# Reordering RWKV's last third and its transposes, one decay multiply, and an identity added on VectorE

## The chip, the cores and the metric

The kernel runs on one core of a Trainium2 chip. The metric is the device time of one execution in microseconds (us), as the median of several. TensorE (PE in the profile) does the matrix products, VectorE (DVE), ScalarE (ACT) and GpSimd (POOL) the rest of the arithmetic; SyncE (SP) only issues transfers.

## What is computed

One layer of a hybrid block over 2048 latent tokens and 256 context tokens, width 1024. An input projection feeds two groups of heads: a bidirectional RWKV-7 mixer with 8 heads of 64, and a multi-head attention with 8 heads. Their gated outputs go through one output projection and are added to the residual stream. The part that the change touches is the RWKV scan, in the reference a loop over tokens, once forward and once backward:

```
def step(S, inp):
    r_t, w_t, k_t, v_t, a_t, b_t = inp
    sa = jnp.einsum('bhij,bhj->bhi', S, a_t)
    S = S * w_t[:, :, None, :] + sa[..., None] * b_t[:, :, None, :] + v_t[..., None] * k_t[:, :, None, :]
    y = jnp.einsum('bhij,bhj->bhi', S, r_t) if emit else None
    return S, y
```

The state of each head is a 64 x 64 matrix; every token decays it (w), applies a delta rule (a, b), adds an outer product (v, k) and reads it out (r).

## The kernel before

The kernel has an input stage (projection, preparation of keys and decays, all stored to DRAM), a stage that projects queries, keys and values for the attention, the attention itself, and the output projection with a final norm.

The RWKV scan is done in 36 chunks of 64 tokens, both directions in one pass (the forward direction in one half of the partitions, the backward one in the other). Within a chunk the token loop is replaced by products: scores between the chunk's keys and receivers (`scores`), the inverse of a unit triangular matrix of 64 x 64 for each head and direction (`inverse`, built by levels with small f16 products), and a chain that carries the state from chunk to chunk (`chain1`, `chain1b`, `chain2`, `chain3`, `chain4`). `transposed` turns a chunk's decayed keys by TensorE transposes against the identity.

This work is laid beside the attention. The attention runs 16 jobs (4 pairs of heads by 4 groups of 512 queries) of 9 macro steps each. A macro step does, for j = 0 to 3, three score products into PSUM (L1426 to L1428), the exponential on ScalarE (L1430), an addition on GpSimd (L1435), some products and maxima for the next job (L1306 on TensorE, L1307 on VectorE), and then one slot of RWKV work (`slot`); after j = 3 a fifth slot follows at once. At its end it calls `tiled`, which is handed the eight products of the step's probabilities with the values (`pv`, L1453) as the function `between`. Three macro steps make one chunk: `tiled` does `chain1`, the second half of the scores and `chain1b` at the end of the first (m = 0), `chain2` at the end of the second (m = 1), `chain3`, `chain4` and the first half of the scores of a later chunk at the end of the last (m = 2). The first 18 macro steps run beside the projection for the attention, and the remaining 99 beside the attention proper.

The inverse of a chunk is a generator; one of its steps runs at each of the slot numbers listed in `STAGES`. Two chunks' inverses overlap. In the first three of its product steps it forms T (here called T0, T1 and T2): T0 in slot 2 of a second macro step, T1 in slot 4 of the same step (right ahead of `between` and `chain2`), T2 in slot 1 of the last macro step. Each is a product of the lower-order matrix with the T before it, plus the identity. The identity comes in through one more product, `self.idt` times `self.id8` (128 x 512, L327), that opens the accumulation in PSUM, and ScalarE copies the sum out (L358). The last inverse step of the older chunk, which makes `Rf` (L393 on VectorE), is in slot 3 of the second macro step, between T0 and T1; `chain2` multiplies by `Rf` (L432).

In the last macro step slot 3 holds the first `level` step (products at L330, two VectorE multiplications at L347), slot 4 another product and its VectorE addition (L370), and `chain3` (products at L446) follows. `chain3` adds to the state on VectorE (L449) and multiplies it by the chunk's decay, one operation for each direction (L451); `chain4` (products at L462) makes the chunk's output (L463).

TensorE's order is the order of the program text (`phase_core` runs under a manual schedule of TensorE). The order of the other engines' queues is made when the program is built, and each queue is then worked through in that order. Products of the inverse and of the chain take their PSUM space from the two banks named "x" (`BANKS`); scores of the attention and the maxima share the three banks named "s". `transposed`, the first half of the scores and `chain1` share one tile of two banks ("bc").

Of the kernel before, what the change touches and what calls it, by code (L numbers as in the profile page):

```python
# [12 lines left out]
ALU = mybir.AluOpType  # L13
# [4 lines left out]
P = 128  # L18
# [52 lines left out]
def bc(ap, n):  # L71

    return ap.unsqueeze(len(ap.shape)).to_broadcast(list(ap.shape) + [n])
# [66 lines left out]
class Rwkv:  # L140
# [67 lines left out]
    def tiled(self, k, between=None):  # L208

        n, m = divmod(k, 3)  # L210
        n -= 3
        ok = lambda i: 0 <= i < self.NC
        between = between or (lambda: None)
        if m == 0:
            between()
            if ok(n):
                self.chain1(n)
            if ok(n + 2):
                self.scores(n + 2, 1)
                self.inv[n + 2] = self.inverse(n + 2)  # L220
                next(self.inv[n + 2])
            if ok(n):
                self.chain1b(n)
            if ok(n + 3):
                self.load_ar(n + 3)
                self.load_bk(n + 3)
        elif m == 1:
            between()
            if ok(n):
                self.chain2(n)  # L230
        else:
            if ok(n):
                self.chain3(n)
                self.chain4(n)
            between()
            if ok(n + 3):
                self.scores(n + 3, 0)

# [42 lines left out]
    def transposed(self, n):  # L281
        nc = self.nc
        tr = self.S[n]["tr"] = []
        pb = self.k.banks.tile([P, 2, 512], F32, name="bc")
        for d in range(2):
            ps = pb[:, d]
            for b in range(4):
                nc.tensor.transpose(ps[:, b * P:(b + 1) * P], self.bk[:, d, b].rearrange("p j t -> p (j t)"), self.k.ident)
            t = self.op.tile([P, 512], F32, name=f"tr{d}", bufs=3)
            (nc.vector.tensor_copy if d else nc.scalar.copy)(t, ps)  # L290
            tr.append(t)

    def scores(self, n, d):
# [24 lines left out]
    def inverse(self, n):  # L318

        nc, s, op, par = self.nc, self.S[n], self.op, n % 2  # L320

        ph, pl = self.bd[f"ph{n % 3}"], self.bd[f"g{par}"]

        def prod(lhsT, rhs, also=None, plus=None):
            ps = self.k.bank("x").rearrange("p (h t) -> p h t", t=64)
            if plus is not None:
                nc.tensor.matmul(ps, self.idt, plus, start=True, stop=False)  # L327
            for h in range(8):
                r = rhs[:, h] if len(rhs.shape) == 3 else rhs
                nc.tensor.matmul(ps[:, h], lhsT[:, h], r, start=plus is None,  # L330
                                 stop=also is None and (plus is None or h == 7))
                if also is not None:
                    nc.tensor.matmul(ps[:, h], also[:, h], r, start=False, stop=plus is None or h == 7)
            return ps

        def packed(name, bufs):
            return op.tile([P, 8, 64], F16, name=f"{name}{par}", bufs=bufs)

        def spread(name, x, both=None):
            for d, ur, vr in self.dirs:  # L340
                (nc.vector.tensor_copy if d and not both else nc.scalar.copy)(self.bd[name][ur, :, ur], x[ur])
            return self.bd[name]

        def level(name, x, i):

            for d, ur, vr in self.dirs:
                nc.vector.tensor_tensor(self.bd[name][ur, :, ur], x[ur],  # L347
                                        self.lvl[ur, i, ur].unsqueeze(1).to_broadcast([64, 8, 64]), op=ALU.mult)
            return self.bd[name]

        pm = op.tile([P, 8, P], F16, name=f"pm{par}")
        nc.vector.tensor_tensor(pm, ph, self.lv8(0), op=ALU.mult)
        T = None
        yield 1
        for i in range(3):
            ps = prod(pm, T if i else self.id64, plus=self.id8)
            T = packed("T", 2)
            nc.scalar.copy(T, ps)  # L358
            if i == 2:
                Dm = packed("D", 1)  # L360
                nc.vector.transpose(Dm, T)
            yield 1
        for lev in (1, 2):
            G = level(f"g{par}", prod(ph, T), lev)
            yield 1
            R = Dm
            for i in range(3):
                ps = prod(G, R)
                R = packed("R", 4)
                nc.vector.tensor_tensor(R, ps, Dm, op=ALU.add)  # L370
                if i == 2:
                    Dm = R
                    if lev == 1:
                        T = packed("T", 2)
                        nc.vector.transpose(T, R)
                    else:
                        Rb = spread("f", R, both=True)
                        for d, ur, vr in self.dirs:
                            nc.gpsimd.tensor_tensor(pl[ur, :, ur], s["sm"][d][ur, :, ur], ph[ur, :, ur],
                                                    op=ALU.subtract)  # L380
                yield 1
        ps = prod(Rb, self.id64)
        T = packed("T", 2)
        nc.scalar.copy(T, ps)
        im = op.tile([P, 8, 64], F16, name="im")
        nc.gpsimd.tensor_tensor(im, self.id8, T, op=ALU.subtract)
        yield 1

        Fb = spread("f", prod(ph, T, also=pl, plus=im))
        yield 1  # L390
        ps = prod(Fb, R)
        Rf = s["R"] = op.tile([P, 8, 64], F32, name="Rf", bufs=2)
        nc.vector.tensor_tensor(Rf, ps, R, op=ALU.add)  # L393
        yield 1
# [41 lines left out]
    def chain3(self, n):  # L436

        nc, s = self.nc, self.S[n]
        if n + 1 >= self.NC:
            return  # L440
        ps = self.k.bank("x").rearrange("p (d b t) -> p d b t", d=2, t=64)
        for b in range(4):
            for d in range(2):
                for hb in range(2):
                    c = slice(64 * (2 * b + hb), 64 * (2 * b + hb) + 64)
                    nc.tensor.matmul(ps[64 * hb:64 * hb + 64, d, b], s["tr"][d][:, c], s["uv"][d][:, c],  # L446
                                     start=True, stop=True)
        st, st2 = self.ST[n % 2], self.ST[(n + 1) % 2]
        nc.vector.tensor_tensor(st2, ps, st, op=ALU.add)  # L449
        for d in range(2):  # L450
            nc.vector.tensor_tensor(st2[:, d], st2[:, d], bc(s["gg"][:, d], 64), op=ALU.mult)  # L451

    def chain4(self, n):

# [1238 lines left out]
```

## Time and profile before

| what | value |
|---|---|
| median of 3 runs | 3074.02 us (3060.97 to 3078.2) |
| the profiled execution's own time | 3086.14 us |
| its span, first to last instruction | 3084.4 us |
| TensorE busy | 2732.8 us, 89% |
| VectorE busy | 1836.6 us, 60% |
| GpSimd busy | 1384.8 us, 45% |
| ScalarE busy | 1287.7 us, 42% |
| mean granted TensorE clock | 0.942 |

The busy time of an engine is the union of its instructions' times. A matrix product's end is modelled, and consecutive products overlap in the pipeline, so what a product costs TensorE is read from the start of one to the start of the next, not from its duration. A line in square brackets gives how long the engine stood idle before an instruction, and what released it. The granted clock is a share of TensorE's full 2.4 GHz; 0.5 is its lower level, 1.2 GHz.

### The profile page before, as it was taken

What the parts mean: (1) busy time and instruction counts of PE and PEld (TensorE: products, weight loads), DVE (VectorE), ACT (ScalarE), POOL (GpSimd) and SP (SyncE); (2) the same over time, 40 slices, a digit from 0 to 9 for tenths busy, and PEclk for the clock granted to TensorE, in tenths of its full rate; (3) what the DMA queues carried; (4) which work ended last, traced back from release to release, by engine and by line L of the source; (5) the groups of instructions that cost most, each with busy time, mean ns of one, the idle gap of its engine ahead of it and who ended that gap; (6) DMA issues with size and microseconds to landing.
All of it is one profiled execution on the core that took longest, in us unless ns stands there. A gap on an engine that the chain in (4) does not pass through costs nothing.

```text
span 3084.4 us, 55159 instructions
## 1 busy us (share of the span) xinstructions
PE 2732.8 (89%) x22035; PEld 2060.9 (67%) x22035; DVE 1836.6 (60%) x2867; ACT 1287.7 (42%) x2245; POOL 1384.8 (45%) x1220
## 2 busy tenths in 40 slices
PE   5999999999998888888888888888888977788998
PEld 3997899987887776556655566565556644444776
DVE  3356834266524576676665766665676757997213
ACT  3446745356523423444443444443444432333221
POOL 2323323333421123566554665554565645776332
PEclk7998999999998998999998999998999986889999
DMA  5224542235545866122132122132221144433443
GB/s 195 80 88 125 147 149 84 84 106 139 164 138 189 270 196 148 44 69 70 50 100 79 59 70 62 56 96 83 71 70 49 39 125 124 123 107 116 147 137 116
DMA packets 409467, 336.66 MB, mean 109 GB/s; under 512 B 130599, under 2 KB 341842, under 8 KB 408186
## 3 DMA queue, kind: packets, MB, share of 16 engines
q1 hardware_dynamic: 405775, 327.19, 36.1%
q8 instruction: 173, 2.83, 0.4%
q0 software_dynamic: 992, 3.21, 0.3%
q10 hardware_dynamic: 2442, 2.73, 0.3%
q14 instruction: 85, 0.69, 0.1%
HBM read 210.68 MB, written 122.31 MB: 108 GB/s over the span
## 4 chain that ended last, share of the span: by engine, by line
PE 45%; DVE 13%; DMA 6%; ACT 5%; issue 3%; POOL 2%; SPq 1%; ACTq 0%; POOLq 0%; DVEq 0%
PE bo L1453 7%; PE bx L1610 6%; PE bs L1426 4%; PE pm L117 4%; DMA x<-s_x 3%; DVE m L1307 3%; PE bs L1306 3%; PE bs L1428 3%; PE bs L1427 3%; ACT pt L1430 2%; PE bx L330 2%; PE bc L406 2%; PE bs L1096 2%; DVE x L251 2%; DVE bdg L347 2%
## 5 line engine op out<-in xcount | busy, mean ns | idle before, releaser
L1435 POOL TENSOR_TENSOR acc<-acc,pt 128x512 f32<-128x512 f32 x512 | 662.3, 1308 | 632.5 <-ACT pt L1430 628.4
L1430 ACT ACTIVATE pt<-bs 128x512 f32<-128x512 f32 x576 | 343.1, 597 | 553.0 <-PE bs L1428 525.7
L1307 DVE TENSOR_REDUCE m<-bs 128x1 f32<-128x512 f32 (+1 forms) x736 | 400.8, 568 | 188.9 <-PE bs L1306 185.2
L1426 PE MATMUL bs<-q,kt 97*128 97x512 f32 x576 | 282.1, 490 | 44.0 <-DVE m L1307 25.6
L1453 PE MATMUL bo<-pt,vt 128*64 128x512 f32 x1152 | 308.9, 659 | 0.0
L548 POOL TENSOR_TENSOR wlo<-wraw,whi 128x1024 fp32r<-128x1024 f32 (+1 forms) x56 | 134.3, 2399 | 265.2 <-PE pm L117 164.4
L1306 PE MATMUL bs<-kt,q 96*128 96x512 f32 (+1 forms) x480 | 182.9, 410 | 62.3 <-ACT pt L1430 31.4
L1428 PE MATMUL bs<-q,kt 97*128 97x512 f32 x576 | 237.3, 412 | 0.0
L1427 PE MATMUL bs<-q,kt 97*128 97x512 f32 x576 | 236.9, 411 | 0.0
L1426 PEld LDWEIGHTS bs<-q,kt 97*128 97x128 f32 x576 | 113.1, 196 | 125.0 <-DVE m L1307 36.6
L1306 PEld LDWEIGHTS bs<-kt,q 96*128 96x128 f32 x480 | 91.6, 191 | 130.5 <-ACT pt L1430 66.2
L132 ACT COPY u<-pm 128x342 f32<-128x342 f32 (+1 forms) x168 | 74.1, 442 | 214.7 <-PE pm L117 214.5
L1453 PEld LDWEIGHTS bo<-pt,vt 128*64 128x64 f32 x1152 | 81.7, 150 | 120.8 <-issue 115.9
L1428 PEld LDWEIGHTS bs<-q,kt 97*128 97x128 f32 x576 | 114.2, 198 | 27.3
L1610 PE MATMUL bx<-wohi,big 128*128 128x512 f32 x496 | 126.0, 394 | 3.9 <-DMA big<-s_mix 3.9
L1427 PEld LDWEIGHTS bs<-q,kt 97*128 97x128 f32 x576 | 115.2, 200 | 4.5
L977 POOL TENSOR_TENSOR xt<-z,nk 128x512 f32<-128x512 f32 (+1 forms) x40 | 53.1, 1329 | 143.6 <-ACT z L976 81.4
L1610 PEld LDWEIGHTS bx<-wohi,big 128*128 128x128 f32 x496 | 93.7, 190 | 25.1 <-issue 4.9
L370 DVE TENSOR_TENSOR R<-bx,R 128x512 f16<-128x512 f32 x108 | 73.6, 682 | 58.4 <-PE bx L330 57.4
L1646 DVE TENSOR_TENSOR acc<-bx,big 128x512 f32<-128x512 f32 x32 | 22.0, 690 | 143.3 <-PE bx L1610 137.9
L825 DVE SCALAR_TENSOR_TENSOR kd<-z,u 128x512 f32<-128x512 f32 x32 | 38.9, 1218 | 111.3 <-ACT z L823 111.3
L347 DVE TENSOR_TENSOR bdg<-bx,lvl 64x512 f16<-64x512 f32 x144 | 98.6, 685 | 5.8 <-PE bx L330 3.2
(320 smaller groups left out, 6431.3 us busy)
## 6 DMA issues: line engine op xcount, KB each, us to landing
wraw<-in_w_in SPq DMA_DIRECT2D x54, 512.0 KB
x<-s_x SPq DMA_DIRECT2D x72, 384.0 KB
s_x<-xt SPq DMA_DIRECT2D x32, 512.0 KB
big<-s_mix SPq DMA_DIRECT2D x24, 512.0 KB
s_kn<-hl SPq DMA_DIRECT2D x36, 256.0 KB
ar<-s_nr SPq DMA_DIRECT2D x72, 128.0 KB
uv<-s_v SPq DMA_DIRECT2D x72, 128.0 KB
s_x<-cum SPq DMA_DIRECT2D x32, 256.0 KB
```

The source lines that it names most:

```text
L117: nc.tensor.matmul(ps[0:m, 0:w], a[:, k, 0:m], x[:, k], start=n == 0, stop=n == 3 * KT - 1)
L347: nc.vector.tensor_tensor(self.bd[name][ur, :, ur], x[ur], self.lvl[ur, i, ur].unsqueeze(1).to_broadcast([64, 8, 64]), op=ALU.mult)
L548: (eng_lo or nc.vector).tensor_tensor(lo, x, hi.bitcast(F32), op=ALU.subtract)
L1306: nc.tensor.matmul(ps[:, 0:w], q[0:96, e, 0, i * P:(i + 1) * P], ks[e], start=True, stop=True)
L1307: nc.vector.tensor_reduce(m5[:, e * NQS + i, j:j + 1], ps[:, 0:w], axis=AX.X, op=ALU.max)
L1426: nc.tensor.matmul(ps, ks[:, e, 0, sl], q[:, e, 0], start=True, stop=False)
L1427: nc.tensor.matmul(ps, ks[:, e, 0, sl], q[:, e, 1], start=False, stop=False)
L1428: nc.tensor.matmul(ps, ks[:, e, 1, sl], q[:, e, 0], start=False, stop=True)
L1430: nc.scalar.activation(pt, ps, AF.Exp, scale=SCALE)
L1435: nc.gpsimd.tensor_tensor(acc[e], held[e] if kt == 1 else acc[e], pt, op=ALU.add)
L1453: nc.tensor.matmul(oo[64 * e:64 * e + 64], VS[j][:, i, 64 * e:64 * e + 64], pts[kt, e], start=kt == 0, stop=kt == NK - 1)
L1610: nc.tensor.matmul(ps, x[:, i], a[:, k, 512 * h:512 * h + 512], start=n == 0, stop=n == last)
```

## The change

Four edits:

1. In the last macro step of a chunk, `tiled` calls `between` (the eight products with the values) ahead of `chain3` and `chain4`, no longer behind them.
2. `transposed` issues all eight transposes first and then the two copies out of PSUM (ScalarE for the first half, VectorE for the second). Before, four transposes and a copy were followed by four transposes and a copy.
3. `inverse` forms T0, T1 and T2 without the identity product; VectorE reads the product from PSUM, adds the identity from SBUF and writes T. ScalarE's copy is gone. The later product that also uses `plus` (with `im`) stays.
4. `chain3` multiplies the state by the decay in one VectorE operation of 128 x 512, where there were two of 128 x 256.

```
@@ tiled @@
         else:
+            between()
             if ok(n):
                 self.chain3(n)
                 self.chain4(n)
-            between()
             if ok(n + 3):
                 self.scores(n + 3, 0)
@@ transposed @@
         for d in range(2):
-            ps = pb[:, d]
             for b in range(4):
-                nc.tensor.transpose(ps[:, b * P:(b + 1) * P], self.bk[:, d, b].rearrange("p j t -> p (j t)"), self.k.ident)
+                nc.tensor.transpose(pb[:, d, b * P:(b + 1) * P], self.bk[:, d, b].rearrange("p j t -> p (j t)"),
+                                    self.k.ident)
+        for d in range(2):
             t = self.op.tile([P, 512], F32, name=f"tr{d}", bufs=3)
-            (nc.vector.tensor_copy if d else nc.scalar.copy)(t, ps)
+            (nc.vector.tensor_copy if d else nc.scalar.copy)(t, pb[:, d])
             tr.append(t)
@@ inverse @@
         for i in range(3):
-            ps = prod(pm, T if i else self.id64, plus=self.id8)
+            ps = prod(pm, T if i else self.id64)
             T = packed("T", 2)
-            nc.scalar.copy(T, ps)
+            nc.vector.tensor_tensor(T, ps, self.id8, op=ALU.add)
@@ chain3 @@
         nc.vector.tensor_tensor(st2, ps, st, op=ALU.add)
-        for d in range(2):
-            nc.vector.tensor_tensor(st2[:, d], st2[:, d], bc(s["gg"][:, d], 64), op=ALU.mult)
+        h64 = lambda t: t.rearrange("p d b t -> p (d b) t")
+        nc.vector.tensor_tensor(h64(st2), h64(st2), bc(s["gg"].rearrange("p d b -> p (d b)"), 64), op=ALU.mult)
```

## Rows read from the trace of the kernel before

**Rows 1.** Windows: busy us (instructions) of PE, PEld, DVE, ACT, POOL; PEclk, DMA, GB/s.

```profile
1220.00:2480.00 1260.00, 1109.41 (x12633) 753.81 (x12630) 845.59 (x1353) 554.84 (x984) 727.52 (x689) 0.96 0.23 66
```

**Rows 2.** Waits of PE from 1220 to 2480 us: total us, times, longest.

```profile
PE bx L446 <- DVE bdg L347: 41.3, 31, 1.7
PE bs L1306 <- ACT pt L1430: 40.2, 67, 2.0
PE bc L288 <- ACT tr L290: 21.4, 30, 0.8
PE bx L432 <- DVE Rf L393: 10.2, 14, 1.1
...
PE bx L432 <- DVE mx L1310: 4.0, 8, 0.6
```

**Rows 3.** Timeline, end of a second macro step: start, duration, engine, operation.

```profile
1783.45 1.40 DVE L347 TENSOR_TENSOR bdg<-bx,lvl 64x512 f16<-64x512 f32 x2
...
1783.82 0.39 PE L327 MATMUL bx<-lvl,idt 128*128 128x512 f16 x1
...
1784.05 0.40 PE L330 MATMUL bx<-lvl,pm 128*128 128x64 f16 x8
...
1784.88 1.99 DVE L251 TENSOR_TENSOR x<-x 128x512 f32<-128x512 f32 x2
...
1785.53 0.40 PE L330 MATMUL bx<-T,pm 128*128 128x64 f16 x8
...
1785.86 1.94 PE L1453 MATMUL bo<-pt,vt 128*64 128x512 f32 x8
...
1786.91 0.76 DVE L1307 TENSOR_REDUCE m<-bs 128x1 f32<-128x256 f32 x2
...
1787.58 0.68 DVE L393 TENSOR_TENSOR Rf<-bx,R 128x512 f32<-128x512 f32 x1
...
1788.41 1.15 PE L432 MATMUL bx<-bt,Rf 64*64 64x64 f32 x32 [0.61 <-DVE mx L1310]
```

**Rows 4.** Timeline, end of a last macro step.

```profile
1831.50 0.39 PE L330 MATMUL bx<-R,bdg 128*128 128x64 f16 x8
...
1831.97 1.39 DVE L347 TENSOR_TENSOR bdg<-bx,lvl 64x512 f16<-64x512 f32 x2
...
1833.51 1.15 PE L446 MATMUL bx<-uv,tr 128*64 128x64 f32 x32 [1.61 <-DVE bdg L347]
...
1835.39 1.92 PE L1453 MATMUL bo<-pt,vt 128*64 128x512 f32 x8
...
1837.24 1.16 PE L307 MATMUL bc<-ar,x 64*128 64x128 f32 x16
```

**Rows 5.** Timeline, the transposes of a chunk.

```profile
1804.43 0.60 PE L288 MATMUL bc<-ident,x 128*128 128x128 f32 x4
...
1805.81 0.66 PE L288 MATMUL bc<-ident,x 128*128 128x128 f32 x4 [0.79 <-ACT tr L290]
...
1806.31 0.40 PE L330 MATMUL bx<-lvl,bdf 128*128 128x64 f16 x8
```

**Rows 6.** One line's instructions, ns: shortest/median/longest of decay (L451) and L251.

```profile
L451 DVE TENSOR_TENSOR st<-st,gg x70: 410/476/1426, 1092.8 to 2461.0; 128x256 f32<-128x256 f32 x70
...
L251 DVE TENSOR_TENSOR x<-x x72: 674/959/1251, 966.9 to 2381.6; 128x512 f32<-128x512 f32 x72
```

**Rows 7.** Timeline, two waits of TensorE elsewhere in the stage.

```profile
1463.80 1.49 PE L446 MATMUL bx<-uv,tr 128*64 128x64 f32 x32 [1.61 <-DVE bdg L347]
...
2144.26 0.79 PE L1426 MATMUL bs<-q,kt 97*128 97x512 f32 x1 [1.81 <-DVE m L1307]
```

**Rows 8.** Windows behind the waits of rows 7 and 4, columns of rows 1.

```profile
1464.40:1467.90 3.50, 3.50 (x55) 2.93 (x53) 2.15 (x4) 1.23 (x2) 1.36 (x2) 0.51 0.02 5
...
2143.60:2150.50 6.90, 6.24 (x29) 3.00 (x29) 2.49 (x7) 1.18 (x2) 3.83 (x4) 0.51 0.22 62
...
1833.50:1840.00 6.50, 6.49 (x101) 4.54 (x101) 4.19 (x8) 1.83 (x3) 1.99 (x2) 1.00 0.29 83
```

## The prediction

> **What bounds the kernel now.** I read the table of windows first, to find the stage that the change touches. The scan runs from about 1000 to 2480 us of the span, from 1220 us on beside the attention. There TensorE is busy for 1109 of 1260 us and VectorE for 846, ScalarE for 555 [rows 1]. So TensorE sets the pace, with some 150 us of idle time, and VectorE is the next engine. The list of TensorE's waits says where that idle time is: 41.3 us ahead of `chain3` (L446) for a `level` step on VectorE, 40.2 us in the maxima for an exponential, 21.4 us between the two halves of the transposes for ScalarE's copy, 14.2 us ahead of `chain2` (L432) in 22 waits for VectorE [rows 2]. The change aims at the first and the third of these. The timeline then shows each place in time: the end of a second macro step [rows 3], the end of a last one [rows 4], the transposes [rows 5]. In rows 3 the reader is to see that VectorE works without a gap from 1783.45 us until `Rf` is done at 1788.26, and that `chain2`, which needs `Rf`, starts right after it: in this place VectorE, not TensorE, sets the pace.
>
> **The change part by part.** The sum is made against the profiled execution, 3086.14 us (span 3084.4 and 1.7 around it), which is 0.4% above the median of 3074.02; I take the difference over to the median unchanged.
>
> *The products with the values ahead of `chain3`.* Today TensorE finishes the product of slot 4 and then waits for the bank that the `level` pair (L347, 1.39 us) still reads: from 1831.50 to 1833.51 there are 2.0 us, 1.61 of them idle [rows 4]. The eight products L1453 take 1.85 us, from 1835.39 to the next line at 1837.24 [rows 4], and need neither bank. Put first, they start about 0.33 us after the last product (as from 1785.53 to 1785.86 in rows 3), at 1831.83, and end at 1833.7, just behind the end of the `level` pair at 1833.36. The wait is covered: 41.3 us in 31 waits [rows 2]. What is late next is VectorE. The state's addition, the decay, the output's addition and the two masks of the scores used to begin while L1453 ran and now all come behind it, directly ahead of the next macro step's maxima. None of the 41.3 us or all of it may come back as waits there; I take a third, 14 us, since these operations together are longer than the 1.85 us of L1453 by about as much as a macro step has idle time on VectorE to absorb. Gain 27 us (0 to 41).
>
> *The transposes.* The first four start at 1804.43, the second four at 1805.81, after 0.79 us idle; the four and what follows them take 0.50 us, up to 1806.31 [rows 5]. Without the wait the second four start 0.50 us after the first: 1.38 - 0.50 = 0.88 us for each of 36 chunks, 32 us (21, the waits of rows 2 alone, to 34). After the change no transpose follows a copy, so the wait can't stay. The two copies come 0.5 us later for ScalarE, and `chain1`, which needs their banks, comes behind the eight products L1453 of 1.85 us; that is the cover, and the copies cost nothing while it stands.
>
> *The identity product.* From the start of L327 to the next product there are 1784.05 - 1783.82 = 0.23 us [rows 3], for 108 of them (three in each of 36 chunks) 25 us of TensorE. The copies leave ScalarE, which has time; I count nothing for that. (At the most it shortens the 40.2 us of waits for an exponential in rows 2.)
>
> *The identity's addition on VectorE.* Its nearest row is L393, an addition from PSUM of the same size: 0.68 us [rows 3]. What matters is where it stands in VectorE's queue. In rows 3 the product for T0 is issued from 1784.05 us. VectorE at that time has ahead of it the `level` pair, then the L251 pair (1.99 us; written a macro step earlier), then two maxima (0.76 us) whose products are written ahead of T0's, then `Rf`. It takes them in the order in which they are written. T0's addition is written behind the maxima and ahead of `Rf`, so I put it where `Rf` now starts: 1787.58 to 1788.26. T1's product, which today starts at 1785.53, needs T0 and waits until about 1788.4, and in TensorE's fixed order L1453 and `chain2` are queued behind it: L1453 0.33 us later at 1788.7, `chain2` 1.85 us after that at 1790.6 in place of 1788.41, 2.2 us late. `Rf`, 0.68 us later than today, is done by then. One chunk in three has one more maximum, of twice the width, behind T0's place, and loses less by it, an estimated 1.6 us. The mean is 2.0 us. It applies where `chain2` today waits for VectorE, which is 14 + 8 = 22 chunks [rows 2]: 44 us (15, if only `Rf` moves, to 73, if all 33 chunks beside the attention lose 2.2). In these 22 the identity products of T0 and T1 save nothing, since VectorE sets the end: 44 x 0.23 = 10 us of the 25 are lost, 15 stay. T2 is made in the last macro step with room around it; its 0.68 us pushes the next addition, on which the product of slot 4 waits, by an estimated third of it: 8 us over 33 chunks (0 to 22).
>
> The Trainium skill speaks against this edit: Perfetto Trace Analysis, section Optimizing Scalar/DVE Operations, says that work of a saturated VectorE may be better off on ScalarE. VectorE's 67% against ScalarE's 44% [rows 1] is far from saturated on average, but rows 3 show a stretch that is. By that rule T stays on ScalarE, and the other three edits alone would give 27 + 32 = 59 us.
>
> *TensorE's clock.* A wait of 1.81 us is followed by 6.9 us with a granted clock of 0.51, one of 1.61 us by 3.5 us at 0.51, another of 1.61 us [rows 4] by none [rows 7, 8]. That is the lower level, 1.2 GHz. T1's new wait is longer than any of these, 2.5 to 2.9 us (from the end of the product ahead of it). A stretch of 3.5 us at 0.51 costs up to 1.7 us of products; part of it lies in the wait itself. I take 1.0 us for each of 22 waits, 22 us (0 to 37).
>
> The skill's page TensorE: Matmul & The Clock Gate, section HAM oscillation, has the same picture: a wait that comes back at each step brings the low clock back at each step. The trace agrees for two of the three waits shown.
>
> *The decay.* Two operations of 0.476 us (median; 0.410 to 1.426) become one of 128 x 512, for which L251 is the nearest row, 0.959 us (0.674 to 1.251) [rows 6]: 0.95 against 0.96, nothing. The bounds per chunk are -0.43 and +2.2 us of VectorE's time; it lies beside TensorE's work, so it enters only by the third above.
>
> *The sum.* Gains 27 + 32 + 15 = 74; losses 44 + 8 + 22 = 74. Nothing is left: 3074 us, the median of before.
>
> **The rivals.**
>
> *Forecast: the gains are eaten by T1's wait.* 3074 us, with its own range 3050 to 3100.
>
> *Rival 1, faster: T0 gets through early.* If VectorE's queue takes T0's addition ahead of the L251 pair, at about 1784.9 in rows 3, T1 never waits; only `Rf` and `chain2` move by 0.68 us, 15 us over 22 chunks, and no long wait lowers the clock. Then 74 - 8 - 15 = 51 us: 3023 us. For it: VectorE's order is made anew for the changed program, and the pair waits for a transfer and an exponential. Against it: in rows 3 the pair runs ahead of maxima whose products were issued before T0's.
>
> *Rival 2, slower: the clock.* One mechanism: each of T1's 22 waits is followed not by 3.5 us but by 6.9 us at the low level, as behind the 1.81 us wait [rows 8], which costs up to 3.4 us and here about 3.0. Then the clock takes 66 us and not 22: 3074 + 44 = 3118 us. It decides from 1.0 us per wait, where the sum is zero; the measurement would tell it from 1.7 us. For it: the new waits are longer than any in rows 4 and 7. Against it: the matrix work behind them is dense.
>
> *That the change doesn't do what it says:* the transposes can't keep their wait, as said; the wait ahead of `chain3` could come back behind L1453, where only 0.3 us separates the two in rows 4. It would cost the 27 us and lead to 3101, within the forecast's edge.
>
> **How the numbers follow.** A measurement of this kernel can tell about 0.5% from no change, 15 us. Forecast 0.55, rival 1 0.25, rival 2 0.20. The range goes from 3005, where rival 1 has the larger gain from `chain3`, to 3112, short of half of rival 2: about 2 in 10 stay outside. Of the forecast a quarter lies over 15 us to either side, because its terms are known to some 25 us together: faster 0.14 + 0.24 = 0.38, same 0.28 + 0.03 = 0.31, slower 0.13 + 0.18 = 0.31.
>
> **What would show it.** In the profile after: L446's wait for L347 gone; no wait in L288 for ScalarE's copy; no L327 but for the `im` product; T's addition at 0.68 us. The deciding line is a wait of TensorE at L330 for the line of T's addition: some 2.5 us in about 22 chunks by the forecast, with VectorE's order L251, maxima, T0, `Rf`; if T0 stands ahead of L251 and that wait is small, rival 1 is right. The granted clock of the stretch from 1220 us, 0.96 today, falls by a few hundredths by the forecast, to about 0.9 by rival 2, and rises by rival 1. The prediction is wrong if VectorE's order in the second macro step is another than I put it, or if the burst at the end of the last macro step gives back much more than a third.

## The result: 0.6% slower, where no change was forecast

The changed kernel takes 3090.8 us (median of 20 runs, 3073.9 to 3110.8) against 3073.6 for the kernel before (median of 20, 3056.0 to 3084.8). The ratio of the means is 1.0063, 95% interval 1.0042 to 1.0084: slower by 0.63%, about 19 us. The range of the forecast holds it, but its likeliest case, that gains and losses cancel, is not what happened. The profiled execution took 3110.8 us (span 3109.0) and is the slowest of the 20, so traces are compared with 25 us between them where the medians differ by 17.

First the stretch from 1220 us in the kernel after, in the columns of [rows 1] (busy time of TensorE, its weight loads, VectorE, ScalarE and GpSimd, then the granted clock):

```profile
1220.00:2480.00 1260.00, 1107.64 (x12292) 751.70 (x12292) 872.06 (x1392) 493.79 (x878) 715.26 (x678) 0.92 0.23 65
```

TensorE is busy as long as in [rows 1], but it gets less done in that time: the granted clock is 0.92 in place of 0.96. The lower level shows as 0.51, so a mean of 0.96 is some 100 us of 1260 at the lower level, and 0.92 some 200.

TensorE's waits in the same stretch (total us, times, longest):

```profile
PE bx L331 <- DVE T L359: 61.7, 24, 6.4
PE bs L1307 <- ACT pt L1431: 36.1, 67, 1.2
PE bx L331 <- DVE R L371: 14.8, 26, 2.5
```

Of [rows 2] the waits ahead of `chain3`, between the transposes and ahead of `chain2` are all gone. In their place stands one new line, T1's product (L331) waiting for T0's addition (L359): 24 waits, 61.7 us, of which 22 last 2.0 to 2.8 us each. (Lines are one higher than before; `Rf` is L394, `chain2` L433, `chain3` L447.)

The end of a second macro step, to be held against [rows 3] (start, duration, engine, line; in brackets the idle time ahead and what ended it):

```profile
1786.82 1.40 DVE L348 TENSOR_TENSOR bdg<-bx,lvl 64x512 f16<-64x512 f32 x2
1787.18 0.41 PE L331 MATMUL bx<-lvl,pm 128*128 128x64 f16 x8
1788.99 1.66 DVE L251 TENSOR_TENSOR x<-x 128x512 f32<-128x512 f32 x2 [0.77 <-ACT x L248]
1789.29 0.41 PE L331 MATMUL bx<-R,bdf 128*128 128x64 f16 x8
1790.68 0.76 DVE L1308 TENSOR_REDUCE m<-bs 128x1 f32<-128x256 f32 x2
1791.35 0.68 DVE L359 TENSOR_TENSOR T<-bx,lvl 128x512 f16<-128x512 f32 x1
1792.05 0.68 DVE L394 TENSOR_TENSOR Rf<-bx,R 128x512 f32<-128x512 f32 x1
1792.09 0.39 PE L331 MATMUL bx<-T,pm 128*128 128x64 f16 x8 [2.38 <-DVE T L359]
1792.41 3.28 PE L1454 MATMUL bo<-pt,vt 128*64 128x512 f32 x8
1795.62 1.43 PE L433 MATMUL bx<-bt,Rf 64*64 64x64 f32 x32
```

T0's product is done early (issued at 1787.18), but VectorE takes the L251 pair and two maxima ahead of T0's addition, as the prediction put it. T1 starts at 1792.09 after 2.38 us of idle time, and the eight products L1454 behind it take 3.28 us; the same eight took 1.94 us in the kernel after where the clock was up (below, at 1840.36). `chain2` comes another 1.3 us late by that.

The table of windows says why, for the wait and two stretches behind it (granted clock is the third number from the end):

```profile
1789.50:1792.90 3.40, 1.01 (x17) 0.57 (x15) 3.37 (x8) 0.60 (x1) 3.40 (x4) 0.99 0.00 0
1792.90:1796.30 3.40, 3.40 (x20) 1.16 (x18) 0.43 (x1) 0.00 (x0) 1.38 (x2) 0.51 0.00 0
1796.30:1800.00 3.70, 3.70 (x54) 2.75 (x51) 1.33 (x2) 2.49 (x5) 0.96 (x1) 1.00 0.03 7
```

During the wait, with TensorE busy for 1.01 of 3.40 us, the clock is still up in this place. It falls when the products have resumed, and stays at 1.2 GHz for 3.4 us in which TensorE is busy without a gap. Beside the attention (from `chain2` of chunk 3, counted from 0, to that of the last chunk, "the stage" below) the trace's records of the clock count 15 such falls with 92 us at the lower level before, and 39 falls with 198 us after. Of the 39, 23 begin in a wait of T1 or within 1.3 us of its end, one for every wait but the shortest; they make 99 of the 198 us, 4.3 us each (17 of them last 3.4 us and 6 last 6.8), and 15 of them begin only after T1's product has started. In the kernel before, 4 of the 31 waits ahead of `chain3` (1.0 to 1.7 us long) had a fall in the same sense.

The end of a last macro step, to be held against [rows 4]:

```profile
1840.03 0.39 PE L331 MATMUL bx<-R,bdg 128*128 128x64 f16 x8 [0.47 <-DVE R L371]
1840.36 1.94 PE L1454 MATMUL bo<-pt,vt 128*64 128x512 f32 x8
1840.50 1.38 DVE L348 TENSOR_TENSOR bdg<-bx,lvl 64x512 f16<-64x512 f32 x2
1842.12 1.10 PE L447 MATMUL bx<-uv,tr 128*64 128x64 f32 x32
1843.99 0.69 DVE L452 TENSOR_TENSOR st<-st,gg 128x512 f32<-128x512 f32 x1
```

L1454 runs while the `level` pair (L348) reads, and `chain3` follows without a wait. The 0.47 us for R, which T2's addition pushes back on VectorE, are the small new cost here.

### The profile page after: what moved, and what is told of

It reads as the page before. It is cut to its first block, busy times and chain, and to the rows that moved or that the text cites. A ratio compares the mean times of both kernels' runs of the same rounds, so it can differ in the third digit from the quotient of the medians.

```text
span 3109.0 us, 54822 instructions
## 1 busy us (share of the span) xinstructions
PE 2754.0 (89%) x21927; PEld 2077.1 (67%) x21927; DVE 1884.7 (61%) x2940; ACT 1226.4 (39%) x2137; POOL 1386.8 (45%) x1220
## 4 chain that ended last, share of the span: by engine, by line
PE 63%; DVE 17%; DMA 6%; ACT 5%; issue 4%; POOL 3%; SPq 1%; ACTq 0%; POOLq 0%; DVEq 0%
PE pm L117 17%; PE bo L1454 9%; PE bx L1611 6%; PE bs L1427 4%; DVE m L1308 3%; PE bs L1307 3%; PE bx L331 3%; PE bs L1429 3%; PE bs L1428 3%; DMA x<-s_x 2%; ACT pt L1431 2%; PE bs L1097 2%; DVE x L251 2%; PE bc L407 2%; PE bx L433 1%
## 5 line engine op out<-in xcount | busy, mean ns | idle before, releaser
L1454 PE MATMUL bo<-pt,vt 128*64 128x512 f32 x1152 | 338.2, 716 | 0.0
L1427 PE MATMUL bs<-q,kt 97*128 97x512 f32 x576 | 286.3, 497 | 49.7 <-DVE m L1308 26.2
L1429 PE MATMUL bs<-q,kt 97*128 97x512 f32 x576 | 240.6, 418 | 0.0
L1428 PE MATMUL bs<-q,kt 97*128 97x512 f32 x576 | 240.4, 417 | 0.0
L1454 PEld LDWEIGHTS bo<-pt,vt 128*64 128x64 f32 x1152 | 83.0, 158 | 135.4 <-issue 128.1
L435 ACT COPY uv<-bx 64x512 f32<-64x512 f32 x72 | 41.8, 580 | 238.8 <-PE bx L433 238.1
```

The source lines that it names most:

```text
L1427: nc.tensor.matmul(ps, ks[:, e, 0, sl], q[:, e, 0], start=True, stop=False)
L1428: nc.tensor.matmul(ps, ks[:, e, 0, sl], q[:, e, 1], start=False, stop=False)
L1429: nc.tensor.matmul(ps, ks[:, e, 1, sl], q[:, e, 0], start=False, stop=True)
L1454: nc.tensor.matmul(oo[64 * e:64 * e + 64], VS[j][:, i, 64 * e:64 * e + 64], pts[kt, e], start=kt == 0, stop=kt == NK - 1)
```

## The experiments

The theory was that the identity's addition on VectorE causes the loss twice over, by T1's wait and by the clock that falls behind it, and that the other three edits gain. The rivals were that the loss lies in the other edits (a burst on VectorE at the end of the last macro step), and that the wait alone costs it, without the clock. Ratios are to the kernel before, run on the same chip.

**All but the identity edit.**

```diff
-            ps = prod(pm, T if i else self.id64)
+            ps = prod(pm, T if i else self.id64, plus=self.id8)
             T = packed("T", 2)
-            nc.vector.tensor_tensor(T, ps, self.id8, op=ALU.add)
+            nc.scalar.copy(T, ps)
```

> The changed kernel without its third edit: T0, T1 and T2 are made as in the kernel before (identity by TensorE, copy by ScalarE); order of the last third, transposes and decay as changed. Theory (T1's wait on VectorE, with the low clock behind it, ate the gains of the other edits): no wait of TensorE for T's line worth naming, falls of the clock beside the attention back to about 15 or fewer, and the gain that the prediction gave to these edits, 59 us: about 3015 us, ratio 0.98. Rival (the other edits never brought that, because VectorE's burst at the end of the last macro step gives it back): 3060 us or more, ratio above 0.995.

Measured: 2999.8 us, ratio 0.9729 (0.9695 to 0.9764). The three edits gain 83 us (73 to 94) where the prediction's terms give 59. The same window as above, and the longest wait for VectorE that is left from [rows 2]:

```profile
1220.00:2480.00 1260.00, 1144.64 (x12852) 782.72 (x12852) 877.44 (x1421) 581.04 (x1033) 772.41 (x720) 0.97 0.26 76
PE bx L433 <- DVE Rf L394: 11.4, 14, 1.1
```

The clock is up at 0.97 (9 falls, 44 us low in the stage). So the identity edit costs 1.0063/0.9729 = 1.034, some 104 us beside the others, and the burst at the end of the last macro step is not the cause.

**The identity edit alone**, in the kernel before.

```diff
-            ps = prod(pm, T if i else self.id64, plus=self.id8)
+            ps = prod(pm, T if i else self.id64)
             T = packed("T", 2)
-            nc.scalar.copy(T, ps)
+            nc.vector.tensor_tensor(T, ps, self.id8, op=ALU.add)
```

> The kernel before with the third edit alone. Theory (the identity edit does all the harm): the waits of TensorE for T's line as in the changed kernel, some 60 us, some 39 falls of the clock beside the attention, and a time well above the changed kernel's, by about the 59 us of the other edits: 3140 to 3150 us, ratio 1.02. Rival (the harm comes from two edits together, as from the products with the values being late): no slower than the changed kernel, 3091 us or less, ratio up to 1.006.

Measured: 3157.1 us, ratio 1.0239 (1.0205 to 1.0272), 73 us slower (63 to 84). The wait is there as in the full change, beside the old ones (TensorE's waits, same stretch):

```profile
PE bx L330 <- DVE T L358: 58.0, 23, 3.0
PE bx L446 <- DVE bdg L347: 38.1, 30, 1.7
PE bc L288 <- ACT tr L290: 20.6, 29, 0.8
```

In the stage there are 37 falls with 212 us at the lower level. The prediction's terms for this edit are 44 + 8 + 22 - 15 = 59 us.

**The wait filled, first try.** Is it the wait or the clock behind it? Ten products that are thrown away, put ahead of T1's into T1's own bank, to keep TensorE busy.

```diff
+            for _ in range(fill):
+                nc.tensor.matmul(ps, self.idt, self.id8, start=True, stop=True)
...
-            ps = prod(pm, T if i else self.id64)
+            ps = prod(pm, T if i else self.id64, fill=10 if i == 1 else 0)
```

> The changed kernel with ten matrix products of 128 x 512 (identity times identity, overwritten) put ahead of T1's product, where TensorE now waits for T0: the wait stays, but TensorE works through most of it, so nothing of the result changes. If the clock is the term that was sized too small (22 us taken): the falls beside the attention go back from 39 to about 15 and with them some 40 us, about 3050 us, ratio 0.993. If it is the wait itself: the falls go down but the time stays within 10 us of the changed kernel's, 3080 us or more, since `chain2` can't start sooner. The ten products take 2.3 us and cost up to 0.5 us in chunks where T0 is early.

Measured: 3159.8 us, ratio 1.0246 (1.0207 to 1.0286). It tells nothing about the clock, as the list of waits shows:

```profile
PE bx L328 <- DVE T L361: 57.5, 23, 3.0
```

L328 is the line of the added products: they themselves wait for T0's addition. The banks "x" go round in two, T0's product, `Rf`'s and T1's take turns, and T1's bank is the one that the addition still reads. The wait stayed and the ten products came behind it, in all 36 chunks.

**The wait filled, second try.** The same idea in a bank of another name, nine products, only in the 23 chunks that have the wait.

```diff
+            if i == 1 and (6 <= n <= 13 or 17 <= n <= 25 or 29 <= n <= 34):
+                fl = self.k.banks.tile([P, 2, 512], F32, name="bc")
+                for _ in range(9):
+                    nc.tensor.matmul(fl[:, 0].rearrange("p (h t) -> p h t", t=64), self.idt, self.id8,
+                                     start=True, stop=True)
             ps = prod(pm, T if i else self.id64)
```

> The changed kernel with nine overwritten matrix products of 128 x 512, identity times identity, ahead of T1's product in the 23 chunks where its trace shows TensorE waiting for T0 (6 to 13, 17 to 25, 29 to 34), now into the two banks that lie free there (those of `chain1`), so that they don't wait for T0 themselves; nothing of the result changes. The nine take about 2.1 us of each wait of 2.4 us. If the low clock behind these waits is what the prediction sized too small: the falls beside the attention go from 39 to about 17, the time at the low level in that stage from 198 us to about 100, and half of that difference, some 45 us, comes off: 3045 us, ratio 0.991. If the waits alone account for the loss: falls go down and the time stays at 3080 us or more, ratio above 1.002.

Measured: 3048.0 us, ratio 0.9909 (0.9877 to 0.9941). Useless work makes the changed kernel 1.5% faster (0.9909/1.0063), some 47 us (35 to 59). The window and the wait:

```profile
1220.00:2480.00 1260.00, 1152.44 (x12955) 782.60 (x12955) 896.05 (x1440) 516.78 (x917) 751.06 (x706) 0.97 0.24 70
PE bx L331 <- DVE T L364: 14.1, 21, 1.0
```

One place in it (the added products are L360, T0's addition is L364, the products with the values L1459):

```profile
1775.92 1.98 DVE L251 TENSOR_TENSOR x<-x 128x512 f32<-128x512 f32 x2
1776.20 2.11 PE L360 MATMUL bc<-lvl,idt 128*128 128x512 f16 x9
1778.60 0.68 DVE L364 TENSOR_TENSOR T<-bx,lvl 128x512 f16<-128x512 f32 x1
1779.33 0.39 PE L331 MATMUL bx<-T,pm 128*128 128x64 f16 x8 [1.02 <-DVE T L364]
1779.65 1.94 PE L1459 MATMUL bo<-pt,vt 128*64 128x512 f32 x8
```

T0's addition still stands behind the L251 pair, and T1 can't start before it; the added products only fill that time. What they bring is the clock: L1459 takes 1.94 us, and in the stage the clock is at 0.97 in place of 0.92, with 13 falls in place of 39 (none of them at a wait of T1) and 79 us low in place of 198. This is the run that decides: T1 still waits for T0's addition and the time comes off all the same, so the fall of the clock at T1's wait costs most of the 47 us, up to 2 per wait.

**T0's addition ahead of the L251 pair**, the order of rival 1, made by hand: the pair is written later, as a function `mul_bk` that `slot` calls, and so comes behind T0's addition and `Rf`.

```diff
+        if m == 1 and j == 3 and 0 <= n + 3 < self.NC:
+            self.mul_bk(n + 3)
...
-        self.bk = x[:, :, :, 1:3]
-        for d in range(2):
-            nc.vector.tensor_tensor(self.bk[:, d], self.bk[:, d], cum[:, d].unsqueeze(2).to_broadcast([P, 4, 2, 64]),
-                                    op=ALU.mult)
+        self.bk, s["cum"] = x[:, :, :, 1:3], cum
...
```

> The changed kernel with the decay of the next chunk's keys (L251, two VectorE multiplications of 128 x 512) issued one slot after T0, in the fourth slot of the second macro step, instead of a macro step earlier. VectorE's queue then has T0's addition and `Rf` ahead of this pair. Theory (T0 is late because this pair stands ahead of it in VectorE's queue): T0 about 2 us sooner, the waits for T's line fall from 62 us to under 10 us, the falls of the clock to 15 or fewer, and `Rf` comes sooner too: about 3010 us, ratio 0.98. Rival (VectorE has too much to do in this macro step in any order): the wait moves to another of its results and the time stays at 3075 us or more.

Measured: 2999.3 us, ratio 0.9735 (0.97 to 0.9771). The waits and the timeline of one place (the moved pair is now L263):

```profile
PE bx L336 <- DVE T L364: 23.8, 34, 1.3
...
1700.32 0.69 DVE L364 TENSOR_TENSOR T<-bx,lvl 128x512 f16<-128x512 f32 x1
1701.06 0.39 PE L336 MATMUL bx<-T,pm 128*128 128x64 f16 x8 [0.22 <-DVE T L364]
1701.38 1.94 PE L1459 MATMUL bo<-pt,vt 128*64 128x512 f32 x8
1701.52 0.68 DVE L399 TENSOR_TENSOR Rf<-bx,R 128x512 f32<-128x512 f32 x1
1702.12 2.62 DVE L263 TENSOR_TENSOR x<-x 128x512 f32<-128x512 f32 x2
```

T1 waits 0.22 us here and L1459 takes its 1.94 us. The waits for T fell from 61.7 us to 23.8, less than expected (they are short ones now, 34 of them), but the clock is back (8 falls, 48 us low in the stage, where TensorE's idle time falls by 45 us). Against the full change (0.9735 against 1.0063) that is some 100 us. The place in VectorE's queue, more than the addition's own 0.68 us, was the cost.

**Order alone, and transposes alone**, in the kernel before.

```diff
         else:
+            between()
             if ok(n):
                 self.chain3(n)
                 self.chain4(n)
-            between()
```

> The kernel before with the first edit alone, the products with the values ahead of `chain3`. The prediction gave it 27 us (0 to 41): about 3047 us, ratio 0.991; TensorE's wait ahead of `chain3` gone, a third of it back as waits in the maxima of the next macro step. If the burst on VectorE gives most of it back: ratio above 0.997. If the falls of the clock that followed that wait go with it: up to 10 us more, ratio 0.988.

Measured: 3039.0 us, ratio 0.9883 (0.984 to 0.9925): 36 us (23 to 49), against 27 in the sum. The wait ahead of `chain3` is gone, and most of what came back are waits for R:

```profile
PE bx L330 <- DVE R L370: 14.0, 19, 1.3
PE bc L288 <- ACT tr L290: 21.3, 30, 0.8
```

The line for R in the kernel before, for comparison:

```profile
PE bx L330 <- DVE R L370: 4.6, 11, 1.1
```

```diff
         for d in range(2):
-            ps = pb[:, d]
             for b in range(4):
...
+        for d in range(2):
             t = self.op.tile([P, 512], F32, name=f"tr{d}", bufs=3)
-            (nc.vector.tensor_copy if d else nc.scalar.copy)(t, ps)
+            (nc.vector.tensor_copy if d else nc.scalar.copy)(t, pb[:, d])
```

> The kernel before with the second edit alone, eight transposes and then two copies. The prediction gave it 32 us (21 to 34): about 3042 us, ratio 0.9895, the wait for ScalarE's copy gone and nothing new in its place. If the stretch behind it is set by VectorE all the same: ratio above 0.996.

Measured: 3036.3 us, ratio 0.9864 (0.982 to 0.9909): 42 us (28 to 55), against 32. The low time in the stage is 68 us here and 92 in the kernel before, but the next run, which gains nothing, has 68 as well: a difference of this size between two single traces shows no effect of an edit.

**The decay alone.**

```diff
-        for d in range(2):
-            nc.vector.tensor_tensor(st2[:, d], st2[:, d], bc(s["gg"][:, d], 64), op=ALU.mult)
+        h64 = lambda t: t.rearrange("p d b t -> p (d b) t")
+        nc.vector.tensor_tensor(h64(st2), h64(st2), bc(s["gg"].rearrange("p d b -> p (d b)"), 64), op=ALU.mult)
```

> The kernel before with the fourth edit alone, one decay multiplication. The prediction gave it nothing (between -0.43 and +2.2 us of VectorE's time per chunk, beside TensorE's work): ratio 0.997 to 1.003. If VectorE's time at the end of the last macro step bounds the next one, it gains up to 0.5 us in each of 36 chunks, 18 us: ratio 0.994.

Measured: 3077.5 us, ratio 0.9984 (0.9959 to 1.0009): nothing that can be told from zero. Its one operation takes 0.69 us (the L452 row above) against 2 x 0.476 [rows 6], better than the equality that the prediction took from L251.

**The three other edits with the L251 pair moved**: the edit of the first experiment and the move of the pair together.

```diff
+        if m == 1 and j == 3 and 0 <= n + 3 < self.NC:
+            self.mul_bk(n + 3)
...
-            ps = prod(pm, T if i else self.id64)
+            ps = prod(pm, T if i else self.id64, plus=self.id8)
             T = packed("T", 2)
-            nc.vector.tensor_tensor(T, ps, self.id8, op=ALU.add)
+            nc.scalar.copy(T, ps)
```

> The kernel of e1 (all edits but the identity's) with the decay of the next chunk's keys (L251) issued in the fourth slot of the second macro step, as in e4. `Rf` no longer stands behind this pair, so the waits of `chain2` (11.4 us beside the attention in e1's trace) go, and the macro step is no longer set by VectorE: 10 to 25 us less than e1, ratio 0.965 to 0.970 against before. Rival: the pair then delays T's successors in the last macro step instead, ratio 0.973 or more as e1.

Measured: 2963.7 us, ratio 0.9639 (0.9598 to 0.968): 3.6% below the kernel before, and no run is faster beyond its interval. No wait for `Rf` is left, and 6 falls with 24 us at the low clock. Against it the kernel with the same pair moved and T0, T1 and T2 on VectorE (0.9735) is 1.0% slower: even with no long wait, these three additions together are better done by TensorE.

**T2 alone on VectorE**, in that version.

```diff
-            ps = prod(pm, T if i else self.id64, plus=self.id8)
+            ps = prod(pm, T if i else self.id64, plus=None if i == 2 else self.id8)
             T = packed("T", 2)
-            nc.scalar.copy(T, ps)
+            if i == 2:
+                nc.vector.tensor_tensor(T, ps, self.id8, op=ALU.add)
+            else:
+                nc.scalar.copy(T, ps)
```

> The kernel of e8 with the third edit for T2 alone (T0 and T1 with the identity by TensorE and ScalarE's copy, T2's identity by VectorE). T2 is made in the last macro step, where VectorE has idle time; it saves 36 products of 0.23 us, 8 us, against 0.68 us of VectorE ahead of the next additions: ratio 0.961 to 0.964 against before if TensorE sets the pace there. If VectorE's queue passes the 0.68 us on to the product of slot 4: 0.964 or more, no better than e8.

Measured: 2973.0 us, ratio 0.9635 (0.9609 to 0.9661), against 0.9639: not to be told apart. The product that T2 saves and the 0.68 us that it adds to VectorE's queue cancel within half a per cent. The price shows as longer waits for R, first without and then with T2 on VectorE:

```profile
PE bx L336 <- DVE R L376: 4.9, 16, 0.4
PE bx L336 <- DVE R L379: 14.8, 26, 1.8
```

## Why the prediction was wrong, step by step

**Where T0's addition stands in VectorE's queue: right.** Behind the L251 pair and two maxima; rival 1 did not happen. T1's wait is 2.0 to 2.8 us in 22 chunks, one of 6.4 and one of 0.2, against "some 2.5 us in about 22 chunks".

**The products ahead of `chain3`: right.** 27 us lies within the interval of the 36 measured. TensorE's idle time in the stage falls by 27 us in that run's trace (150.6 to 123.3), so of the 41.3 us [rows 2] a third came back, as forecast. Some 9 of it are waits for R (14.0 less the 4.6 of before), which is not the place that the prediction named.

**The transposes: right.** 32 us lies within the interval of the 42 measured; the stage is 34 us shorter in the trace. The eight transposes now run in one stretch:

```profile
1810.90 1.04 PE L287 MATMUL bc<-ident,x 128*128 128x128 f32 x8
1811.97 0.59 ACT L291 COPY tr<-bc 128x512 f32<-128x512 f32 x1 [0.22 <-PE bc L287]
```

**These edits together: too small.** With the decay they gain 83 us (73 to 94), and 59 lies outside. TensorE's idle time in the stage falls by 54 us with them; beside it the low time falls from 92 to 44 us, some 19 to 24 us of work by the price worked out below, for which the sum had no term. The runs agree: their median granted clock is 0.950 against 0.943 for the kernel before.

**T1's wait, T2 and the identity product: about right.** TensorE's idle time in the stage goes from 96.5 us without the identity edit to 154.4 with it: 58 us, against 44 + 8 = 52. The waits for R that T2 adds are some 10 us in the last experiment, against 8. The product itself was priced at 25 us, 15 of them kept.

**TensorE's clock: the step that failed.** The prediction took 1.0 us for each of 22 waits, 22 us. What a microsecond at the lower level costs can be estimated in two ways. In the trace after, the transposes (L287) start 109 ns apart at the upper level and 213 at the lower (medians), so at most half of the low time is lost. And among the 20 executions of the changed kernel, whose granted clock goes from 0.923 to 0.934, one with 1 us more of low time (worked out from its clock) took about 0.4 us longer. At 0.4 to 0.5, the 99 us low at T1's 23 waits cost 40 to 50 us, 1.7 to 2.2 per wait; the filled wait gave some 47 independently (of the 119 us of low time that it took away, 20 were away from T1). That is about twice the 1.0 taken.

Two things were wrong inside the step. The prediction set part of the 3.5 us of [rows 8] inside the wait, although 15 of the 23 falls begin only after T1's product has started, and 6 of them last twice as long. It also left out that the low time also rises away from T1: from 44 us in the first experiment to 198 - 99 = 99 us here, 22 to 27 us of work that the sum did not hold (rough, since it compares one execution of each kernel). All in all the identity edit adds 154 us of low time, 62 to 77 us of work against 22. With the idle time and the product saved that makes 58 + 62 - 25 = 95 to 58 + 77 - 25 = 110 us, where the stage became 105 us longer between the two traces (1180.9 to 1285.7).

That three waits stood for all was weak evidence: two of the three shown in [rows 7] and [rows 4] have a fall behind them, but only 4 of the 31 ahead of `chain3` do, and no more than two of the waits that the kernel before has in this stage are as long as T1's shorter ones. The trace of before could not price a wait of 2.0 to 2.8 us.

**Rival 2 had the mechanism.** Its point of decision was 1.0 us per wait, and 1.7 to 2.2 were measured; its price of 3.0 was too high, since most of the falls last 3.4 us and not 6.9. "The matrix work behind them is dense", which the prediction set against it, spoke for it: dense work is what a low clock slows. Its terms for the identity edit, 44 + 8 + 66 - 15 = 103 us, meet the 104 measured partly by luck: its 66 us were for T1's waits alone, which cost 40 to 50.

**Luck.** That the forecast of 3074 us came within 17 us is luck: the identity edit was priced at 59 us and cost 104, the other edits at 59 and gained 83, and the two errors are of opposite sign.

The Trainium skill's rule that the prediction weighed (Perfetto Trace Analysis, section Optimizing Scalar/DVE Operations), by which T stays on ScalarE, turned out to be the better forecast for T0 and T1: the kernel made by it is the first experiment, 0.9729, with a gain of 83 us where the prediction priced that case at 59. For T2 alone it made no difference (0.9635 against 0.9639).

**Open.** One wait of T1, in chunk 33, lasted 6.4 us. There T0's addition stood behind an L251 pair of 5.51 us, where the pair shown above took 1.66:

```profile
2358.60 5.51 DVE L251 TENSOR_TENSOR x<-x 128x512 f32<-128x512 f32 x2
2364.75 0.68 DVE L359 TENSOR_TENSOR T<-bx,lvl 128x512 f16<-128x512 f32 x1
```

Why the pair took so long is not shown. Of the 16 falls that are not at T1, several follow waits of about half a microsecond in the maxima of the first macro step; why there are more of them than in the first experiment is not shown either.

## What to carry to other kernels

In a stage that TensorE bounds, a new wait of some 2 us has two prices, its own length and the low clock behind it. Three examples don't give the second: count, for waits of each length, how many have a fall and how long it lasts (here 4 of 31 for 1.0 to 1.7 us, every one of 22 for 2.0 to 2.8 us), and where the trace before has no waits of the new length, time that edit alone. When work is moved to another engine, what decides is not that engine's mean load (67% here) but what stands ahead of the moved operation in its queue: the same additions of 0.68 us cost 104 us with T0's behind a pair of 1.7 to 2 us, and some 30 us once the pair was out of its way. Edits that take out waits and an edit that adds one are best timed apart: together they came out as 0.6% slower, and hid a gain of 2.7%.

## What the runs showed that was not expected

Nine products that nobody reads, 23 times over, made a kernel 1.5% faster, some 47 us, by keeping the granted clock at 0.97 in place of 0.92. The price of a fall also did not add up from one edit to the next: the identity edit alone raised the low time from 92 to 212 us and cost 73 us, but on top of the other edits, which had brought it down to 44, it raised it to 198 and cost 104.
